# More units of a two-layer MLP computed with joined 512-column passes

## The chip, the cores and the metric

The kernel runs on 1 core of one Trainium2 chip. The metric is the device time of one execution in microseconds (us). Three executions of the kernel before took 1423.88, 1424.63 and 1425.09 us; the median is 1424.63 us.

The engines are called PE (TensorE: matrix products), PEld (its weight loads), DVE (VectorE), ACT (ScalarE), POOL (GpSimd) and SP (SyncE, which issues transfers).

## The reference

The program is a decoder trunk of two layers over 512 tokens of 1024 channels, all in float32. Each layer has a token mixer (a recurrence with pooling in the first, a Conformer convolution in the second), a cross-attention into 256 memory tokens, and a gated MLP. The change concerns the MLP:

```python
def conv_ffn(x, norm, w_up, dw_w, dw_b, w_down):
    h = rms_norm(x, norm) @ w_up                 # 1024 -> 2 * 3072
    g = causal_dwconv(h[..., :D_FF], dw_w, dw_b) # width 3, along the tokens
    u = h[..., D_FF:]
    return (jax.nn.gelu(g) * u) @ w_down         # 3072 -> 1024

for layer in range(DEPTH):                       # DEPTH = 2
    x = x + mixer(x); x = x + cross_attn(x, mem); x = x + conv_ffn(x)
return rms_norm(x, final_norm)
```

## The kernel before

**Split operands.** A float32 number is held as two parts, a rounded high part and the rest (low). A product of a weight block and an activation is three matmuls that add into one PSUM bank: high weight by high activation, high weight by low activation, low weight by high activation (`mm3`, L187 to L189).

**Units.** The up projection of the MLP makes 24 pairs of 128 channels, one gate row and one value row each; a pair is called a unit, c = 0 to 23. Units 0 and 1 are plain. Units 2 to 23 use a seven-product scheme (Strassen's, in Winograd's form): the 512 tokens are halved into two times 256, the 1024 input channels into two times 512, and seven products of a 128x512 weight block with a 512x256 activation block take the place of eight. The weight blocks are named a11, a12, a22, s1, s2, s3, s4 (the s are sums of blocks); the activation blocks are B11, B21, B22 and four combinations T1 to T4. The products add into three PSUM tiles: G takes a11 and a12; F takes a copy of a11's result (L992) and then s2, s3 and a22; H takes s1 and s4. Between two products ACT and DVE take the running value of F out of the bank.

On PE the order of a unit c is: s1, s2, a12, s3, then the down projection for units that were finished four to seven units ago (24 matmuls of 512 columns into tiles named `aux`, from unit 4 on), then a11 of the next unit (`ahead`), then s4 and a22. Units 2 and 3 have no down projection between s3 and a11.

**Narrow and joined products.** In a narrow unit each product is 12 matmuls of 256 columns: for each of four 128-channel chunks the three of `mm3`. In a joined unit (the code says wide, `WIDE` at L42) the products into F and G are made in `product` (L817) with 8 matmuls: for each chunk one of 512 columns, the high weights by the high and low activations side by side, and one of 256 columns, the low weights by the high activations. The two column halves of the bank are added afterwards (`gather`, L955 on ACT and L172 on DVE). H has 256 columns in both cases, and lies in the tile `stat` in joined units, in a tile `mm` in narrow ones.

**The re-laying copies.** A joined product needs the high and the low half of an activation block side by side. T1 to T4 are built so. B11, B21 and B22 are not; ACT re-lays them once a layer with copies of 128x256 (L217, four per block). `put_aside` first copies the high half of B22 to a spare place (4 copies), `put_beside(B21)` then writes the low half of B21 where B22's high half stood, `put_beside(B22)` puts B22 together, and `put_beside(B11)` does B11. From `put_aside` on, the product s4 reads B22's high half from the spare place. Where these calls stand is set by `WIDE[0]`, the first joined unit: aside and B11 two units ahead of it, B21 and B22 one unit ahead.

**Order.** Within the MLP the order of PE, ACT, DVE and POOL is the order of the code (`manual_schedule`). `finish`, which ends the second layer (down projection of the last four units in 384 columns, final norm), is ordered by the framework's scheduler up to its last part. The end of unit 23 is a chain on DVE and ACT: F and H times the norm (L963, L931 narrow; L961, L969 joined), convolution (L939, L942 twice), gelu (L944), product with the value row (L976), split (L979 high, L981 low). `finish` then multiplies the last result.

Of the kernel before, what the change touches and what calls it, by code (L numbers as in the profile page):

```python
# [24 lines left out]
CF = D_FF // P  # L25
# [13 lines left out]

KE = 2  # L40
PARKED = 4
WIDE = range(6, 22)  # L42
READY = 8
WINDOWS = (2, 4, 8, 16)

# [17 lines left out]
def trunk(ctx: ExitStack, tc: tile.TileContext, I: dict, out: list):  # L63
# [32 lines left out]
    def tmp_f(n=T):  # L96
        return tmp.tile([P, n], F32, tag="tmp", name=nm("tmp"))
# [73 lines left out]
    def add(out, a, b):  # L171
        V.tensor_tensor(out, a, b, op=ALU.add)  # L172
        return out
# [703 lines left out]
        return {c: Blocks(I["wpair"][layer * (CF - PLAIN) + c - PLAIN]) for c in range(PLAIN, CF)}  # L877

    def ffn(layer, norm, nxt, seven, pairs):
        ys = {}  # L880

        class Down:

# [11 lines left out]
            def bank(self, i, seeded):  # L895

                ps = aux_ps()
                if seeded:
                    A.activation(ps, X[2 * self.j + i], AF.Copy)
                return ps  # L900
# [16 lines left out]
        def high(c, name):  # L917
            if c in pairs and (c, name) not in done:
                pairs[c].high(name)

        def low(c, name):
            if c in pairs and (c, name) not in done:
                pairs[c].low(name)
                done.add((c, name))

        def both(c, name):
            high(c, name)
            low(c, name)

        def times_r(out, ps, at):  # L930
            V.tensor_tensor(out[:, at], ps, norm.r[:, at], op=ALU.mult)  # L931
# [13 lines left out]
            yield y  # L945

        def wide(c):
            return c in WIDE

        def bank(c):  # L950
            return main_ps() if wide(c) else main_ps()[:, :M]

        def gather(out, ps):

            A.activation(out, ps[:, M:], AF.Copy)  # L955
            add(out, ps[:, :M], out)
# [26 lines left out]
        def m(c, ps, block, j, first=True):  # L983
            seven.product(ps, pairs[c].w[block], j, first)

        def ahead(c):

            G, F = bank(c), bank(c)
            m(c, G, "a11", seven.B11)
            if c == WIDE[0] + 1:  # L990
                PE.matmul(F, pairs[c].w["a11"][0][:, :P], seven.both(seven.B11, 0), start=True, stop=True)
            A.activation(F, G, AF.Copy)  # L992
            return G, F

        def unit(c):

            nonlocal left, chains
            G, F = chains
            down, seeded = downs.get(c), c > GC
            H = (stat_ps if wide(c) else main_ps)()[:, :M]  # L1000
            m(c, H, "s1", seven.T1)
            if c <= second:
                high(c + 1, "s3")
            next(left, None)
            if c <= second:
                low(c + 1, "s3")

            m(c, F, "s2", seven.T2, False)
            u, f, g = tmp_f(), tmp_f(), tmp_f()
            if wide(c):  # L1010
                gather(u[:, :M], F)
            else:
                A.activation(u[:, :M], F, AF.Copy)
            if c == first:
                both(c + 2, "a11")
            if down:
                d = [down.bank(i, seeded) for i in range(2)]
            next(left, None)
            both(c + 1, "s3")
            next(left, None)  # L1020
            high(c + 1, "a22")

            m(c, G, "a12", seven.B21, False)
            next(left, None)
            next(left, None)
            high(c, "s4")
            if c == second:
                high(c + 2, "a11")
            low(c, "s4")
            if wide(c):  # L1030
                gather(g[:, left_half], G)
            elif c > second:
                times_r(g, G, left_half)

            m(c, F, "s3", seven.T3, False)
            if wide(c):
                gather(u[:, M:], F)
            else:
                A.activation(u[:, M:], F, AF.Copy)
            add(f[:, right_half], H, u[:, M:])  # L1040
            if c <= second:
                times_r(g, G, left_half)
            if c == second:
                low(c + 2, "a11")
            low(c + 1, "a22")
            if not wide(c):
                V.tensor_tensor(f[:, right_half], f[:, right_half], norm.r[:, right_half], op=ALU.mult)
            both(c + 2, "a11")
            high(c + 1, "a12")
            low(c + 1, "a12")  # L1050
            if c == WIDE[0] - 2:
                seven.put_aside()
            elif c == WIDE[0] - 1:
                seven.put_beside(seven.B21)
            if down:
                for ks in (range(GC - 1), (GC - 1,)):
                    for i in range(2):
                        down.products(i, d[i], seeded, ks)
            if c + 3 in pairs:
                pairs[c + 3].load()  # L1060
            if c + 2 in pairs and c > first:
                pairs[c + 2].load_second()
            if c > second and c + 1 in downs:
                downs[c + 1].w.high()
                downs[c + 1].w.low()
            if c + 2 in downs and first < c <= CF - 2:
                downs[c + 2].load()
            high(c + 1, "s1")
            low(c + 1, "s1")
            high(c + 1, "s2")  # L1070
            low(c + 1, "s2")
            if c == second:
                downs[c + 1].w.high()
                downs[c + 1].w.low()
            if down:
                down.home(0, d[0], seeded)

            if c + 1 in pairs:
                chains = ahead(c + 1)
            if down:  # L1080
                down.home(1, d[1], seeded)
            if c == WIDE[0] - 2:
                seven.put_beside(seven.B11)

            m(c, H, "s4", seven.B22, False)
            m(c, F, "a22", seven.T4, False)
            if c == WIDE[0] - 1:
                seven.put_beside(seven.B22)
            left = gating(c, g, f, u, F, H)
            next(left)  # L1090

        def opening():
# [67 lines left out]

            start(3)
            chains = ahead(first)

            def rest():
# [14 lines left out]
        with tc.manual_schedule(engines=ORDERED):  # L1179
            opening()  # L1180
            for c in range(PLAIN, CF):
                unit(c)
            for _ in left:
                pass
# [714 lines left out]
    six = mixer(n0, n1)  # L1899
    pairs = pairs_of(0)  # L1900
    mem, parked = ffn(0, n2, n3, attention(0, n1, mem, n2, six, pairs[PLAIN]), pairs)
    six = conformer(n3, n4, mem, parked)
    pairs = pairs_of(1)
    ffn(1, n5, None, attention(1, n4, mem, n5, six, pairs[PLAIN]), pairs)


# [76 lines left out]
```

## Time and profile before

| What | Value |
|---|---|
| median of three executions | 1424.63 us |
| the profiled execution, its own time | 1424.63 us |
| its span, first to last instruction | 1422.8 us |
| PE busy | 1411.7 us, 99% |
| ACT busy | 934.0 us, 66% |
| DVE busy | 1115.0 us, 78% |
| granted clock of PE, mean | 0.999 of full speed |

The span is 1.8 us shorter than the time. The busy time of PE counts matmuls from start to a modelled end, and they overlap in the pipeline, so 99% says that PE has few gaps and not that it could not issue faster. How closely matmuls follow each other is read from their start times. The MLP of the first layer lies between 340 and 620 us of the span, that of the second from 1040 us on.

### The profile page before, as it was taken

The numbers are of one execution on the slowest core, as the hardware profiler recorded it, in microseconds if no ns is written. First come the engines' busy times: TensorE is split into PE (matmuls) and PEld (weight loads), VectorE is DVE, ScalarE is ACT, GpSimd is POOL, SyncE is SP. The second block draws the span as 40 slices with busy tenths as digits, with TensorE's granted clock in tenths as the row PEclk, the third lists the DMA queues.
The fourth block names the chain that finished last, engine by engine and source line by source line (L and its number), as shares of the span: only waits on it lengthen the run. The fifth ranks groups of instructions, "written<-read, shape, count | busy, mean of one in ns | idle before, by whom it ended". The sixth has DMA issues, their size and how long they took to land.

```text
span 1422.8 us, 21779 instructions
## 1 busy us (share of the span) xinstructions
PE 1411.7 (99%) x8012; PEld 1228.3 (86%) x8012; DVE 1115.0 (78%) x1860; ACT 934.0 (66%) x1688; POOL 316.8 (22%) x333
## 2 busy tenths in 40 slices
PE   9999999999999999999999999999999999999998
PEld 7988888998898888888988777899889888888897
DVE  6987776778877777777798997968788777777775
ACT  7578744777576676666665547766756766666664
POOL 0011310110122222222008993011002222222211
PEclk9999999999999999999999999999999999999999
DMA  8623232544387777776442454345438777777741
GB/s 302 198 75 103 91 118 82 114 116 135 97 205 168 173 172 170 171 173 168 134 133 89 119 158 153 105 88 133 112 98 193 180 176 165 176 174 167 175 122 60
DMA packets 80027, 204.26 MB, mean 144 GB/s; under 512 B 9008, under 2 KB 9520, under 8 KB 79920
## 3 DMA queue, kind: packets, MB, share of 16 engines
q1 hardware_dynamic: 50832, 150.15, 32.5%
q0 software_dynamic: 28800, 52.44, 21.5%
q8 instruction: 63, 1.03, 0.3%
q14 instruction: 44, 0.36, 0.1%
q10 hardware_dynamic: 288, 0.27, 0.1%
HBM read 145.16 MB, written 2.10 MB: 103 GB/s over the span
## 4 chain that ended last, share of the span: by engine, by line
PE 92%; DVE 2%; POOL 2%; DMA 1%; issue 1%; ACT 1%; SPq 0%; POOLq 0%; DVEq 0%; ACTq 0%
PE mm L817 16%; PE mm L187 15%; PE mm L188 15%; PE mm L189 15%; PE aux L187 7%; PE aux L188 7%; PE aux L189 7%; PE stat L187 2%; PE stat L189 2%; PE stat L188 2%; PE mm L465 2%; DMA raw<-in_wv 1%; POOL actf L1583 1%; DVE wlo L168 1%; PE aux L539 0%
## 5 line engine op out<-in xcount | busy, mean ns | idle before, releaser
L188 PE MATMUL mm<-act,whi 128*128 128x512 f32 (+2 forms) x805 | 296.8, 369 | 0.3 <-DVE act L182 0.2
L187 PE MATMUL mm<-act,whi 128*128 128x512 f32 (+2 forms) x805 | 296.6, 370 | 0.6 <-ACT act L281 0.6
L189 PE MATMUL mm<-act,wlo 128*128 128x512 f32 (+2 forms) x805 | 296.6, 368 | 0.0
L187 PEld LDWEIGHTS mm<-act,whi 128*128 128x128 f32 x805 | 151.5, 188 | 26.8 <-ACT act L281 0.9
L188 PEld LDWEIGHTS mm<-act,whi 128*128 128x128 f32 x805 | 151.7, 188 | 26.0 <-DVE act L168 1.0
L189 PEld LDWEIGHTS mm<-act,wlo 128*128 128x128 f32 x805 | 151.6, 188 | 25.1 <-DVE wlo L168 0.6
L866 DVE TENSOR_TENSOR bigr<-raw,bigr 128x512 fp32r<-128x512 f32 x176 | 120.7, 687 | 61.0 <-ACT bigr L859 57.3
L187 PE MATMUL aux<-act,whi 128*128 128x512 f32 x399 | 155.6, 390 | 0.0
L188 PE MATMUL aux<-act,whi 128*128 128x512 f32 x399 | 155.5, 390 | 0.0
L189 PE MATMUL aux<-act,wlo 128*128 128x512 f32 x399 | 155.3, 389 | 0.0
L859 ACT ACTIVATE bigr<-raw 128x512 fp32r<-128x512 f32 x176 | 109.4, 623 | 68.7 <-DVE wlo L204 66.2
L872 POOL DMA_DIRECT2D raw<-wa x100 | 87.3, 893 | 299.7 <-DVE bigr L866 189.8
L167 ACT ACTIVATE whi<-raw 128x1024 fp32r<-128x1024 f32 (+1 forms) x95 | 96.5, 1020 | 85.8 <-PE mm L188 45.7
L817 PE MATMUL mm<-bigr,bigr 128*128 128x512 f32 (+1 forms) x768 | 150.6, 338 | 0.0
L817 PEld LDWEIGHTS mm<-bigr,bigr 128*128 128x128 f32 x768 | 118.3, 189 | 14.3
L869 POOL DMA_DIRECT2D raw<-raw x50 | 43.2, 864 | 371.6 <-DVE wlo L866 297.6
L172 DVE TENSOR_TENSOR tmp<-mm,tmp 128x256 f32<-128x256 f32 x194 | 77.8, 417 | 40.4 <-ACT tmp L955 37.9
L168 DVE TENSOR_TENSOR wlo<-raw,whi 128x1024 fp32r<-128x1024 f32 (+1 forms) x75 | 90.3, 1209 | 19.0 <-ACT whi L167 18.3
L817 PE MATMUL mm<-act,whi 128*128 128x512 f32 x256 | 95.5, 396 | 0.0
L189 PEld LDWEIGHTS aux<-act,wlo 128*128 128x128 f32 x399 | 74.9, 188 | 15.9
L188 PEld LDWEIGHTS aux<-act,whi 128*128 128x128 f32 x399 | 74.9, 188 | 15.5
L187 PEld LDWEIGHTS aux<-act,whi 128*128 128x128 f32 x399 | 75.0, 188 | 14.2
(378 smaller groups left out, 3505.5 us busy)
## 6 DMA issues: line engine op xcount, KB each, us to landing
raw<-wa POOLq DMA_DIRECT2D x150, 256.0 KB, 3.4
wa<-in_wpair SPq DMA_DIRECT2D x88, 256.0 KB, 3.8
raw<-in_wpair SPq DMA_DIRECT2D x44, 512.0 KB, 3.8
big<-in_wdown SPq DMA_DIRECT2D x42, 512.0 KB, 4.6
raw<-raw POOLq DMA_DIRECT2D x50, 256.0 KB, 4.1
raw<-in_pw SPq DMA_DIRECT2D x24, 512.0 KB, 3.4
raw<-in_win SPq DMA_DIRECT2D x20, 512.0 KB, 3.3
raw<-in_wk SPq DMA_DIRECT2D x16, 512.0 KB, 3.3
```

The costliest lines, as they stand in the source:

```text
L167: A.activation(hi, src, AF.Copy)
L168: fetched[1] = (eng or V).tensor_tensor(lo, src, hi.bitcast(F32), op=ALU.subtract)
L172: V.tensor_tensor(out, a, b, op=ALU.add)
L187: PE.matmul(ps, wh, xh, start=first, stop=False, skip_group_check=onto)
L188: PE.matmul(ps, wh, xl, start=False, stop=False, skip_group_check=onto)
L189: return PE.matmul(ps, wl, xh, start=False, stop=last, skip_group_check=onto)
L465: PE.matmul(p, m[j], x, start=k == 0 and j == 0 and x is hi, stop=k == C - 1 and x is lo)
L817: PE.matmul(to, part, by, start=first and c == 0 and i == 0, stop=c == 3 and i == 1, skip_group_check=True)
L859: A.activation(self.w[name][0], self.block(name), AF.Copy)
L866: V.tensor_tensor(lo, self.block(name), hi.bitcast(F32), op=ALU.subtract)
L869: G.dma_start(self.r, self.z, accum_op=ALU.add)
L872: G.dma_start(block, self.a22, accum_op=ALU.add)
```

## The change

`WIDE` becomes one range per layer. Unit 5 becomes a joined one in both layers, and units 22 and 23 also in the second layer. So four units change from narrow to joined, and the re-laying copies, whose place follows `WIDE[0]`, move from units 4 and 5 to units 3 and 4. One matmul that opens a bank moves from unit 7's a11 to unit 6's.

```diff
-WIDE = range(6, 22)
+WIDE = range(5, 22), range(5, CF)
...
-        ys = {}
+        ys, wides = {}, WIDE[layer]
...
         def wide(c):
-            return c in WIDE
+            return c in wides
...
-            if c == WIDE[0] + 1:
+            if c == wides[0] + 1:
                 PE.matmul(F, pairs[c].w["a11"][0][:, :P], seven.both(seven.B11, 0), start=True, stop=True)
...
-            if c == WIDE[0] - 2:
+            if c == wides[0] - 2:
                 seven.put_aside()
-            elif c == WIDE[0] - 1:
+            elif c == wides[0] - 1:
                 seven.put_beside(seven.B21)
...
-            if c == WIDE[0] - 2:
+            if c == wides[0] - 2:
                 seven.put_beside(seven.B11)
...
-            if c == WIDE[0] - 1:
+            if c == wides[0] - 1:
                 seven.put_beside(seven.B22)
```

The first place where the order changes is ACT in unit 3 of the first layer. The names: `whi_3801` is unit 4's a12, `bigr_3984` and `bigr_3987` (in the changed kernel `bigr_3990`, `bigr_3993`) are unit 4's s1 and s2, `mm_3996` is F of unit 4. Before:

```order
L1039 ACTIVATE tmp_3925<-mm_3850 128x256
L859 ACTIVATE whi_3801<-wa_3651 128x512
L859 ACTIVATE bigr_3984<-raw_3647 128x512
L859 ACTIVATE bigr_3987<-raw_3647 128x512
L201 ACTIVATE whi_3991<-big_3653 128x1024
L992 ACTIVATE mm_3996<-mm_3995 128x256
L939 ACTIVATE tmp_4036<-tmp_3927,par 128x512
```

The same place in the changed kernel:

```order
L1039 ACTIVATE tmp_3925<-mm_3850 128x256
L859 ACTIVATE whi_3801<-wa_3651 128x512
L217 ACTIVATE act_3976<-act_3264 128x256
L217 ACTIVATE act_3976<-act_3337 128x256
L217 ACTIVATE act_3977<-act_3438 128x256
L217 ACTIVATE act_3977<-act_3540 128x256
L859 ACTIVATE bigr_3990<-raw_3647 128x512
L859 ACTIVATE bigr_3993<-raw_3647 128x512
L201 ACTIVATE whi_3997<-big_3653 128x1024
L992 ACTIVATE mm_4002<-mm_4001 128x256
L217 ACTIVATE act_3251<-act_3252 128x256
L217 ACTIVATE act_3297<-act_3298 128x256
```

The four copies of `put_aside` stand behind a12's split, and those of B11 behind the copy of a11's result.

PE in the same unit: the product s4 of unit 3 (`mm_3892` is H, `bigr_3949` the weight block), with the semaphores that an instruction waits for. Before:

```order
L189 MATMUL mm_3995<-act_3500,wlo_3802 128x256
L187 MATMUL mm_3892<-act_3264,bigr_3949 128x256 [waits DVE_49]
L188 MATMUL mm_3892<-act_3265,bigr_3949 128x256
L189 MATMUL mm_3892<-act_3264,bigr_3949 128x256
L187 MATMUL mm_3892<-act_3337,bigr_3949 128x256
L188 MATMUL mm_3892<-act_3338,bigr_3949 128x256
```

In the changed kernel:

```order
L189 MATMUL mm_4001<-act_3500,wlo_3802 128x256
L187 MATMUL mm_3892<-act_3976,bigr_3949 128x256 [waits DVE_49,Activation_49]
L188 MATMUL mm_3892<-act_3265,bigr_3949 128x256
L189 MATMUL mm_3892<-act_3976,bigr_3949 128x256
L187 MATMUL mm_3892<-act_3976,bigr_3949 128x256 [waits Activation_49]
L188 MATMUL mm_3892<-act_3338,bigr_3949 128x256
L189 MATMUL mm_3892<-act_3976,bigr_3949 128x256
L187 MATMUL mm_3892<-act_3977,bigr_3949 128x256 [waits Activation_49]
```

It now reads the copies, and each chunk has a wait for ACT of its own.

The third place is the end of the second layer on ACT (`tmp_14417`, in the changed kernel `tmp_14351`, is unit 23's gate row; L1222 takes transposed channels of x out of PSUM for `finish`). Before:

```order
L904 ACTIVATE x<-aux_14322 128x512
L939 ACTIVATE tmp_14417<-tmp_14318,par 128x512
L944 ACTIVATE tmp_14417<-tmp_14417 128x512
L1222 ACTIVATE big_14450<-aux_14480 128x512
L979 ACTIVATE act_14424<-tmp_14417 128x512
```

In the changed kernel:

```order
L904 ACTIVATE x<-aux_14267 128x512
L939 ACTIVATE tmp_14351<-tmp_14262,par 128x512
L955 ACTIVATE tmp_14261<-mm_14199 128x256
L1222 ACTIVATE big_14386<-aux_14416 128x512
L944 ACTIVATE tmp_14351<-tmp_14351 128x512
L979 ACTIVATE act_14360<-tmp_14351 128x512
```

A gather has come in, and L1222 has moved ahead of the gelu.

On PE, at the same end, `finish` reads the last result (`act_14424`, in the changed kernel `act_14360`) for the first time after the four transposes of L1221. Before, seven matmuls stand between:

```order
L1221 MATMUL aux_14480<-ident,x 128x128 x4
L187 MATMUL mm_14492<-act_14011,whi_14431 128x384
L188 MATMUL mm_14492<-act_14012,whi_14431 128x384
L189 MATMUL mm_14492<-act_14011,wlo_14432 128x384
L187 MATMUL mm_14492<-act_14180,whi_14431 128x384
L188 MATMUL mm_14492<-act_14181,whi_14431 128x384
L189 MATMUL mm_14492<-act_14180,wlo_14432 128x384
L187 MATMUL mm_14492<-act_14338,whi_14431 128x384
L187 MATMUL mm_14451<-act_14424,whi_14385 128x384
L187 MATMUL mm_14467<-act_14424,whi_14385 128x384
L188 MATMUL mm_14492<-act_14339,whi_14431 128x384
```

In the changed kernel eighteen stand there, nine into `mm_14428` and nine into `mm_14445`; these are the last of them and what follows:

```order
L187 MATMUL mm_14445<-act_14137,whi_14367 128x384
L188 MATMUL mm_14445<-act_14138,whi_14367 128x384
L189 MATMUL mm_14445<-act_14137,wlo_14368 128x384
L187 MATMUL mm_14387<-act_14360,whi_14323 128x384
L187 MATMUL mm_14403<-act_14360,whi_14323 128x384
L187 MATMUL mm_14428<-act_14360,whi_14367 128x384
L187 MATMUL mm_14445<-act_14279,whi_14367 128x384
L188 MATMUL mm_14387<-act_14361,whi_14323 128x384
```

The first matmul with the last result stands eleven matmuls later than before.

## Rows read from the trace of the kernel before

**Rows 1.** The page: busy time by engine, and the chain's shares by engine.
```profile
PE 1411.7 (99%) x8012; PEld 1228.3 (86%) x8012; DVE 1115.0 (78%) x1860; ACT 934.0 (66%) x1688; POOL 316.8 (22%) x333
...
PE 92%; DVE 2%; POOL 2%; DMA 1%; issue 1%; ACT 1%; SPq 0%; POOLq 0%; DVEq 0%; ACTq 0%
```

**Rows 2.** Stretches: length, busy time (instructions) per engine, granted clock, DMA share, GB/s.
```profile
404.92:420.46 15.54, 15.54 (x110) 14.58 (x109) 11.80 (x21) 11.80 (x26) 3.44 (x4) 1.00 0.84 189
451.43:466.77 15.34, 15.34 (x89) 13.50 (x88) 11.80 (x21) 10.40 (x21) 3.44 (x4) 1.00 0.66 162
1365.95:1381.49 15.54, 15.54 (x111) 14.58 (x109) 10.41 (x18) 8.38 (x16) 1.72 (x2) 1.00 0.40 102
```

**Rows 3.** Timeline of PE, units 4 and 5: start, duration (us), instruction.
```profile
410.39 0.28 PE L187 MATMUL mm<-act,whi 128*128 128x256 f32 x1
...
420.46 0.40 PE L187 MATMUL aux<-act,whi 128*128 128x512 f32 x1
```

**Rows 4.** Timeline of ACT, unit 3 of the first layer.
```profile
395.56 0.62 ACT L859 ACTIVATE whi<-wa 128x512 fp32r<-128x512 f32 x1
396.09 0.62 ACT L859 ACTIVATE bigr<-raw 128x512 fp32r<-128x512 f32 x1
397.92 0.63 ACT L859 ACTIVATE bigr<-raw 128x512 fp32r<-128x512 f32 x1 [1.22 <-PE mm L189]
...
399.41 0.37 ACT L992 ACTIVATE mm<-mm 128x256 f32<-128x256 f32 x1
401.75 0.81 ACT L939 ACTIVATE tmp<-tmp,par 128x512 f32<-128x512 f32 x1 [1.98 <-DVE tmp L963]
```

**Rows 5.** Timeline of ACT, unit 4: copies and what follows them.
```profile
409.11 1.33 ACT L217 ACTIVATE act<-act 128x256 fp32r<-128x256 f32 x4
410.34 1.05 ACT L201 ACTIVATE whi<-big 128x1024 fp32r<-128x1024 f32 x1
```

**Rows 6.** Groups of DVE by line and form: count, busy us, mean ns, idle before.
```profile
L961 DVE TENSOR_TENSOR tmp<-tmp,r 128x512 f32<-128x512 f32 x32 | 22.1, 692 | 1.1
...
L963 DVE TENSOR_TENSOR tmp<-tmp,r 128x256 f32<-128x256 f32 x12 | 5.1, 424 | 0.4
```

**Rows 7.** Timeline of all engines where s4 of unit 3 begins, first layer.
```profile
395.70 0.42 DVE L172 TENSOR_TENSOR tmp<-mm,tmp 128x256 f32<-128x256 f32 x1
...
396.18 0.19 PEld L187 LDWEIGHTS mm<-act,bigr 128*128 128x128 f32 x1
396.18 0.39 PE L187 MATMUL mm<-act,bigr 128*128 128x256 f32 x1
```

**Rows 8.** The same place in the second layer.
```profile
1080.36 0.19 PEld L187 LDWEIGHTS mm<-act,bigr 128*128 128x128 f32 x1
```

**Rows 9.** Timeline of PE in `finish`.
```profile
1394.44 0.94 PE L187 MATMUL mm<-act,whi 128*128 128x384 f32 x3
1395.22 0.33 PE L188 MATMUL mm<-act,whi 128*128 128x384 f32 x1
1395.39 0.33 PE L189 MATMUL mm<-act,wlo 128*128 128x384 f32 x1
```

**Rows 10.** Timelines of ACT and DVE at the end of unit 23, second layer.
```profile
1390.17 0.81 ACT L939 ACTIVATE tmp<-tmp,par 128x512 f32<-128x512 f32 x1 [1.60 <-DVE tmp L963]
1394.08 0.62 ACT L979 ACTIVATE act<-tmp 128x512 fp32r<-128x512 f32 x1
...
1391.02 1.54 DVE L942 SCALAR_TENSOR_TENSOR tmp<-tmp,par,tmp 128x511 f32<-128x511 f32 x2 [0.55 <-ACT tmp L939]
```

**Rows 11.** Timelines of DVE, ACT and PE in joined unit 20, second layer.
```profile
1347.01 1.53 DVE L942 SCALAR_TENSOR_TENSOR tmp<-tmp,par,tmp 128x511 f32<-128x511 f32 x2
1348.45 0.42 DVE L172 TENSOR_TENSOR tmp<-mm,tmp 128x256 f32<-128x256 f32 x1
...
1344.83 0.82 ACT L939 ACTIVATE tmp<-tmp,par 128x512 f32<-128x512 f32 x1 [0.33 <-DVE tmp L961]
...
1349.06 0.74 PE L817 MATMUL mm<-bigr,bigr 128*128 128x512 f32 x3
```

## The prediction

> **What bounds the kernel now.** I read the page first. PE is busy 1411.7 us of 1422.8, and the chain that ended last runs for 92% through PE [rows 1]. So the question is how fast PE issues, and which waits open a gap on it. Next I read the stretches that hold one unit each, from the first matmul of one unit's down projection to the first of the next [rows 2]. In all of them PE is busy the whole time at a granted clock of 1.00, that is 2.4 GHz, while ACT is busy 8.38 to 11.80 us and DVE 10.41 to 11.80 us of some 15.4. ACT and DVE have slack on average, PE has none: a unit lasts as long as PE takes to issue its matmuls. A narrow unit takes 15.54 us in either layer, a joined one 15.34. The timeline gives the same at finer grain: 84 matmuls of 256 columns start between 410.39 and 420.46 [rows 3], one every 0.120 us. Last I looked for the places where the changed order lets PE wait: s4 of unit 3, and the first use of the last result in `finish`.
>
> **Part 1: four units become joined.** Each loses 20 matmuls (five products of 12 become five of 8); the columns streamed stay 3072 a product. The load counts of the stretches, 109 against 88, show these 20 and one instruction of the stretch's edge [rows 2]. The worth is 15.54 - 15.34 = 0.20 us a unit; unit 5 twice and units 22 and 23 once make 4 x 0.20 = 0.80 us. It cannot be much more, as the columns remain. The added work is three gathers (ACT and DVE) and wider multiplications by the norm. It costs nothing inside units 5 and 22, because joined units with the same additions already run with PE busy throughout. If that cover were gone it would show as rival 3.
>
> Here a rule speaks against the change. The rows give 0.20 us for 20 matmuls, or 10 ns for one left out. The Trainium skill (TensorE: Matmul & The Clock Gate, "Wait — 56ns, not 53.3ns?") says that a warm matmul takes its columns at 2.4 GHz and about 2.5 ns more. By that rule 20 matmuls fewer would be worth 0.05 us a unit, 0.2 us in all, an estimate from that page; the trace does not agree with it for these loads and shapes, as 0.120 us for 256 columns leaves 13 ns above 107. The sum goes by the rows; the rule is rival 4.
>
> **Part 2: the copies one unit sooner.** In units 4 and 5 they had time: a down projection stands between s3 and s4 there. In unit 3 none does, and s4 now reads what `put_aside` writes. On ACT the copies stand behind a12's split (395.56, 0.62 us); the instruction after it started at 396.09 [rows 4], so the first copy starts there. Four copies take 1.33 us and the next instruction starts 1.23 us after the first [rows 5]: one starts every 0.31 us, and the first lasts 1.33 - 3 x 0.31 = 0.41 us. So it ends at 396.50.
>
> PE loads s4's first weights at 396.18 before the change [rows 7]. This was itself the end of a wait: the DVE instruction that reads H (395.70, 0.42 us) ended at 396.12, and the load followed 0.06 us later. With the same 0.06 us the load comes at 396.56, which is 0.38 us later. The next chunk follows 3 x 0.12 = 0.36 us behind, its copy only 0.31 us, so each later chunk finds its copy ready: I take one wait of 0.38 us. The second layer has the same pattern (load at 1080.36) [rows 8]. Together +0.76 us. Bounds: nothing, if ACT runs somewhat ahead of PE there; and 1.3 us a layer, if PE waits for the fourth copy. I take 0.38 because the changed order gives each chunk its own wait.
>
> What the copies push: the split of s1 (396.09) moves 1.23 us back, but ACT sat idle for 1.22 us after it, so the split of s2 at 397.92 stays [rows 4]. s1's block is read only after s4 and a22, 24 matmuls or 2.9 us after s4's start. The four copies of B11 fit into ACT's idle 1.98 us before L939 [rows 4]. Behind PE's new wait queue all later matmuls, a loss that nothing gives back, since PE has no slack. SP and POOL keep their order; no transfer is added. Unit 4 keeps eight copies, now B21's and B22's, in the places of those it had; unit 5 loses its eight.
>
> **Part 3: the end.** Before, `finish` waits for the last result: three matmuls of 384 columns take 1395.22 - 1394.44 = 0.78 us where the pitch is 0.17 [rows 9], a loss of 0.26 us. L979 made that operand by 1394.70 [rows 10]. The joined end is a longer chain. L961 takes 0.69 us against 0.42 for L963 [rows 6]: +0.27. From L939 to L942 it takes 1347.01 - 1344.83 = 2.18 us in a joined unit [rows 11] against 1391.02 - 1390.17 = 0.85 us at the narrow end [rows 10], for the gather waits behind L939 on ACT: +1.33. So the operand comes 1.60 us later, near 1396.3. But its first use stands eleven matmuls later in the changed order, 11 x 0.17 = 1.9 us. The wait should shrink from 0.26 us to little; I take -0.20. Bounds: -0.26, and +0.30 if the chain grows by 0.56 us more than I think (L1222, now ahead of the gelu, could do that, though the transposes that it waits for come well before the gelu's input).
>
> **Sum.** -0.80 + 0.76 - 0.20 = -0.24 us on the profiled execution, whose own time of 1424.63 us is the median of the three. That gives 1424.4 us, with 1424.0 to 1424.9 as this case's own range.
>
> **Rivals.**
>
> 1. The copies are hidden, ACT being early enough, so that s4 doesn't wait longer. Then -0.80 - 0.20 = -1.0: 1423.6 us. For it: the wait is 0.38 us only, little against the spread of an instruction's start. Against: both layers show the same pattern with PE and ACT level to a tenth of a us [rows 4, 7, 8].
> 2. The other side: s4 of unit 3 waits for the last copy and not the first. The copies end at 396.09 + 1.33 = 397.42, the load comes at 397.48, 1.3 us late, in two layers 2.6 us: -0.80 + 2.6 - 0.20 = +1.6, or 1426.2 us. It decides from 0.5 us a layer on, where the wait eats the 1.0 us of gains. For it: ACT might start the copies late if a12's split is late. Against: the waits stand chunk by chunk.
> 3. The chains of joined units collide. In unit 20 DVE ends the gather of F at 1348.45 + 0.42 = 1348.87, and s3, which writes that bank again, starts at 1349.06 [rows 11]: some 0.1 us to spare. Units 6, 22 and 23 now run behind a joined unit, four places over both layers. If each waits 0.25 us, the sum is -0.24 + 1.0: 1425.4 us. Against: units 8 to 21 run so already without a gap.
> 4. The joined passes are worth less than the stretches say, because most of the 0.20 us between them comes from something else, such as fewer copies and splits on the memories beside PE. If a quarter is left, -0.2 + 0.76 - 0.20 = +0.36, or 1425.0 us. Against: the narrow stretch of unit 22's end has ACT and DVE far less busy (8.38 and 10.41 us) than that of unit 4's (11.80 both), and both take 15.54 us [rows 2]. The rule of the Trainium skill in Part 1 (TensorE: Matmul & The Clock Gate) would leave about that quarter.
>
> **How the numbers follow.** Chances: forecast 0.56, rival 1 0.12, rival 2 0.15, rival 3 0.10, rival 4 0.07. The three executions of before spread from 1423.88 to 1425.09, so a median can move by some 0.4 us by itself. The range is 1423.1 to 1426.2 us: it takes in rivals 1, 3 and 4 with that spread, and reaches rival 2. About what a measurement of this kernel can tell from no change is 0.2%, 2.8 us. No case reaches it; only several errors of one sign would. Faster 0.03, within 0.94, slower 0.03.
>
> **What would show it.** In the changed profile: 80 matmuls fewer; stretches of units 5 (both layers), 22 and 23 (second layer) of 15.34 instead of 15.54 us; in unit 3 of each layer the first weight load of s4 about 0.06 us behind the end of the first L217 and some 0.4 us later than its place in the stream of matmuls; no other new gap on PE in the two MLPs; and in `finish` hardly a gap where the last result is first used. I am wrong if s4 of unit 3 waits over 0.5 us or not at all, if PE gaps appear before s3 of units 6, 22 or 23, or if the end of `finish` is late by more than 0.3 us.

## The result, and the profile after

The changed kernel takes 1429.42 us, the median of 7 runs (1426.64 to 1430.19), against 1424.45 us of the kernel before, run beside it (7 runs, 1423.05 to 1425.09). The ratio is 1.0034, with an interval of 1.0025 to 1.0043: 5 us slower, where 0.2 us faster was forecast. The profiled execution took 1426.64 us, the fastest of the seven, 2.0 us more than the one of before. So 3 of the 5 us are not in this profile.

The page of the changed kernel, busy times and the chain's shares [rows 1]:

```profile
PE 1410.6 (99%) x7932; PEld 1223.7 (86%) x7932; DVE 1120.2 (79%) x1868; ACT 937.0 (66%) x1696; POOL 316.8 (22%) x333
...
PE 85%; DVE 4%; issue 3%; DMA 3%; ACT 2%; POOL 2%; SPq 0%; POOLq 0%; ACTq 0%; DVEq 0%
```

80 matmuls went and PE is busy 1.1 us less, but the span grew: PE idles 3.2 us more. The chain leaves PE oftener (85% against 92%), and DMA and "issue" grow in it. The stretches [rows 2] from the down projection of unit 4 to that of unit 5 in the first layer, and from that of unit 22 to that of unit 23 in the second (both took 15.54 us before):

```profile
404.41:419.80 15.39, 15.39 (x94) 13.72 (x93) 12.06 (x22) 11.77 (x26) 3.44 (x4) 1.00 0.84 191
...
1366.53:1381.87 15.34, 15.34 (x89) 13.55 (x88) 11.80 (x20) 9.20 (x18) 1.72 (x2) 1.00 0.42 105
```

So the joined units run nearly as forecast: 15.34 to 15.39 us at a full clock. Where s4 of unit 3 begins, first PE, then ACT [rows 4, 7]:

```profile
395.19 0.28 PE L189 MATMUL mm<-act,wlo 128*128 128x256 f32 x1
395.67 0.39 PE L187 MATMUL mm<-act,bigr 128*128 128x256 f32 x1 [0.20 <-ACT act L217]
395.89 0.28 PE L188 MATMUL mm<-act,bigr 128*128 128x256 f32 x1
```
```profile
394.69 0.62 ACT L859 ACTIVATE whi<-wa 128x512 fp32r<-128x512 f32 x1
395.21 1.33 ACT L217 ACTIVATE act<-act 128x256 fp32r<-128x256 f32 x4
396.43 0.63 ACT L859 ACTIVATE bigr<-raw 128x512 fp32r<-128x512 f32 x1
```

The next matmul starts 0.48 us after the one ahead instead of 0.12: 0.36 us, once a layer, for the first copy alone. The first use of the last result in `finish` [rows 9, 10], PE and then ACT:

```profile
1396.18 0.34 PE L189 MATMUL mm<-act,wlo 128*128 128x384 f32 x1
1397.10 0.62 PE L187 MATMUL mm<-act,whi 128*128 128x384 f32 x2 [0.58 <-ACT act L979]
```
```profile
1387.81 1.06 ACT L167 ACTIVATE whi<-raw 128x1024 fp32r<-128x1024 f32 x1 [0.32 <-DMA raw<-in_wdown]
...
1396.42 0.63 ACT L979 ACTIVATE act<-tmp 128x512 fp32r<-128x512 f32 x1 [0.76 <-DVE tmp L976]
```

The wait did not shrink; it grew from 0.26 to 0.85 us, and ahead of it ACT waits for a load of down weights. Transfers are late elsewhere too. The issues by group (count, KB each, median us from issue to landing), before and after:

```profile
raw<-in_win SPq DMA_DIRECT2D x20, 512.0 KB, 3.3
raw<-in_wk SPq DMA_DIRECT2D x16, 512.0 KB, 3.3
...
last<-big SPq DMA_DIRECT2D x1, 256.0 KB, 2.3
last<-big ACTq DMA_DIRECT2D x1, 256.0 KB, 2.6
```
```profile
raw<-in_win SPq DMA_DIRECT2D x20, 512.0 KB, 3.7
raw<-in_wk SPq DMA_DIRECT2D x16, 512.0 KB, 3.7
...
last<-big SPq DMA_DIRECT2D x1, 256.0 KB, 3.5
last<-big ACTq DMA_DIRECT2D x1, 256.0 KB, 3.7
```

Loads that the change does not touch take 0.4 us longer, and the two last stores some 1.1 us longer. By the start of the same PE instruction in both traces, the profiled difference of +2.0 us is made up so:

| stretch | us |
|---|---|
| start, first attention (waits for first loads, -1.0 to +1.2 among the profiles without idle matmuls at the start) | -0.87 |
| first MLP (one wait of 0.36 us; joined unit -0.17) | +0.24 |
| last down weights of the first MLP, matmul at 712 us | +0.59 |
| conformer, second attention | +0.21 |
| second MLP (waits of 0.36 and 0.39 us; joined units) | +0.21 |
| end of `finish`: the last result | +0.63 |
| from there to the end: the last stores | +1.00 |

The ACT row behind the third line, after the change; before, the idle time ahead was 1.41 us:

```profile
708.45 1.06 ACT L167 ACTIVATE whi<-raw 128x1024 fp32r<-128x1024 f32 x1 [2.00 <-DMA raw<-in_wdown]
```

### The profile page after: what moved, and what is told of

Read it like the earlier page. It is cut to its first block, busy times and chain, and to the rows that moved or that the text cites. A ratio compares the mean times of both kernels' runs of the same rounds, so it can differ in the third digit from the quotient of the medians.

```text
span 1424.9 us, 21640 instructions
## 1 busy us (share of the span) xinstructions
PE 1410.6 (99%) x7932; PEld 1223.7 (86%) x7932; DVE 1120.2 (79%) x1868; ACT 937.0 (66%) x1696; POOL 316.8 (22%) x333
## 4 chain that ended last, share of the span: by engine, by line
PE 85%; DVE 4%; issue 3%; DMA 3%; ACT 2%; POOL 2%; SPq 0%; POOLq 0%; ACTq 0%; DVEq 0%
PE mm L817 17%; PE mm L187 12%; PE mm L188 12%; PE mm L189 12%; PE aux L187 7%; PE aux L188 7%; PE aux L189 7%; PE stat L187 2%; PE stat L189 2%; PE stat L188 2%; PE mm L465 2%; DMA raw<-in_wv 1%; DVE wlo L168 1%; DMA raw<-wa 1%; ACT whi L167 1%
## 5 line engine op out<-in xcount | busy, mean ns | idle before, releaser
L187 PE MATMUL mm<-act,whi 128*128 128x512 f32 (+2 forms) x773 | 287.2, 373 | 1.7 <-ACT act L979 1.1
L188 PE MATMUL mm<-act,whi 128*128 128x512 f32 (+2 forms) x773 | 287.8, 372 | 0.3 <-DVE act L182 0.2
L189 PE MATMUL mm<-act,wlo 128*128 128x512 f32 (+2 forms) x773 | 287.5, 372 | 0.0
L817 PE MATMUL mm<-bigr,bigr 128*128 128x512 f32 (+1 forms) x864 | 169.5, 339 | 0.1
L187 PEld LDWEIGHTS mm<-act,whi 128*128 128x128 f32 x773 | 145.4, 188 | 27.9 <-ACT act L979 1.9
L188 PEld LDWEIGHTS mm<-act,whi 128*128 128x128 f32 x773 | 145.6, 188 | 25.9 <-DVE act L168 1.0
L189 PEld LDWEIGHTS mm<-act,wlo 128*128 128x128 f32 x773 | 145.5, 188 | 25.0 <-DVE wlo L168 0.6
L817 PEld LDWEIGHTS mm<-bigr,bigr 128*128 128x128 f32 x864 | 133.0, 189 | 16.5 <-DVE tmp L172 0.4
L172 DVE TENSOR_TENSOR tmp<-mm,tmp 128x256 f32<-128x256 f32 x202 | 80.9, 417 | 43.2 <-ACT tmp L955 41.4
L817 PE MATMUL mm<-act,whi 128*128 128x512 f32 x288 | 107.4, 396 | 0.0
L955 ACT ACTIVATE tmp<-mm 128x256 f32<-128x256 f32 x144 | 49.8, 371 | 67.5 <-PE mm L817 67.5
L188 PEld LDWEIGHTS aux<-act,whi 128*128 128x128 f32 x399 | 74.9, 188 | 15.7
```

The lines of the kernel that those rows point to most:

```text
L187: PE.matmul(ps, wh, xh, start=first, stop=False, skip_group_check=onto)
L188: PE.matmul(ps, wh, xl, start=False, stop=False, skip_group_check=onto)
L189: return PE.matmul(ps, wl, xh, start=False, stop=last, skip_group_check=onto)
L817: PE.matmul(to, part, by, start=first and c == 0 and i == 0, stop=c == 3 and i == 1, skip_group_check=True)
```

## The experiments

Each changes one or two places of the changed kernel or of the kernel before. "From 30 us on" below means the span's difference to the profile of before, less the difference that was there at 30 us; it is +3.0 us for the changed kernel's profile.

**e1 to e4: the parts.** Unchanged again; the sixth units alone; the last two alone; unit 22 alone.

```diff
-WIDE = range(5, 22), range(5, CF)
+WIDE = range(5, 22), range(5, 22)     # e2
+WIDE = range(6, 22), range(6, CF)     # e3
+WIDE = range(6, 22), range(6, 23)     # e4
```

> The changed kernel once more, unchanged, for a second profile beside its times. Theory A (the end of the second layer: the joined last unit makes a longer chain, and the last transfer of the down weights and the last gather stand in it): the profile shows a PE gap of 1 us or more before the first use of the last result in finish, and the time is 1427 to 1430 us. Theory B (unit 5: joined behind an unseeded unit 4, s3 waits for the gather on DVE, and the copies wait at s4 of unit 3): gaps of 0.3 to 1.5 us at s4 of unit 3 and s3 of unit 5 in both layers, which vary from run to run, and the end as in the first profile.

> Only unit 5 joined in both layers (and the copies one unit sooner); units 22 and 23 of the second layer stay narrow. Theory A: the loss is in the end, so this one takes 1424.5 to 1425.2 us (two waits of 0.4 us, one of 0.4 us at s3 of unit 5, less 0.4 us of gain). Theory B: it takes most of the loss, 1427 to 1429 us.

> Only units 22 and 23 of the second layer joined; unit 5 narrow and the copies where they were. Theory A: 1427 to 1429.5 us, with the PE gap in finish. Theory B: 1424.0 to 1425.0 us (0.4 us of gain, 0.6 us of wait at the end).

> Only unit 22 of the second layer joined, unit 23 narrow, unit 5 narrow. Theory A (it is the chain of the last unit that costs): as before or 0.2 us faster, 1424.2 to 1424.6 us, and the end of the trace as before. If joined unit 22 itself costs (its gathers stand in unit 23, where the weights for finish are split): 1425.5 us or more.

Against 1424.33 of before: e1 1428.91 (ratio 1.002 to 1.0045), e2 1425.56 (0.9997 to 1.0014), e3 1423.82 (0.9987 to 1.0005), e4 1424.14 (0.999 to 1.0008). Neither part carries the excess: +1.2 and -0.5 alone (neither clear of the scatter), +4.6 together. Both theories fell. In e2 and e3 the loads of in_wk take 3.4 and 3.3 us and the last store 2.3 and 2.8; the 2.8 us of e3 stay open, as no instruction fetch falls into that store.

**e5, e6: the sixth unit of one layer, with the last two.** `range(5, 22), range(6, CF)` and `range(6, 22), range(5, CF)`.

> The sixth unit joined in the first layer alone, the last two of the second layer as in the changed kernel. Alone, the two sixth units cost +1.2 us (1425.56 against 1424.33) and the last two gave -0.5 (1423.82), together +4.5. Theory E (place of an instruction fetch: in the changed kernel the 8 KB fetch of queue 14 that starts 1421.71 shares a DMA engine with the packets of the last store, which end 1422.67; ACT and DVE have 8 and 9 instructions more, so it falls earlier than in the kernels that add 4): with 6 and 7 more it falls between, about 1 us behind the last store; the store is not delayed and the time is 1424 to 1425 us. Theory F (the second layer's sixth unit and the last two hinder each other): no such pair here, 1424 to 1424.6 us. Theory G (either layer's sixth unit does it): half of the excess, 1426 to 1427 us.

> The second layer alone changed: sixth unit and last two joined, the first layer as before. Theory E (place of an instruction fetch): the same 6 and 7 instructions more as with the first layer's sixth unit, so the same time as that kernel within 0.5 us, 1424 to 1425 us, and the last store not delayed. Theory F (the second layer's sixth unit and the last two hinder each other): the whole excess is here, 1428 to 1429.5 us. Theory G: half of the excess, 1426 to 1427 us.

1427.07 (1.001 to 1.0027) and 1426.11 (1.0005 to 1.0023). The last store is in time (2.4 us in both), as theory E said, but both are 1 to 2 us slower than it allows, whichever layer: the loads are long (3.8 and 3.7 us) in both.

**e7, e8: moving the last fetch.** In the changed kernel an instruction fetch of 8 KB starts at 1421.71, and the last store's packets that should end near 1421.9 end at 1422.67. The transfers between 1421.3 and 1423 us by queue (packets, MB, share of 16 DMA engines):

```profile
q10 hardware_dynamic: 98, 0.17, 28.0%
q1 hardware_dynamic: 24, 0.02, 3.0%
q14 instruction: 1, 0.01, 1.1%
```

```diff
             left = gating(c, g, f, u, F, H)
             next(left)
+            if layer == 0 and 10 <= c < 18:
+                A.activation(pad, eps, AF.Copy)     # e7; e8: V.tensor_copy(pad, eps)
```

Here and below `pad` stands for a spare tile of one column.

> The changed kernel with 8 more instructions on ACT, copies of one column into a spare tile, one in each of units 10 to 17 of the first layer, where ACT is busy 12 of 15 us. They compute nothing that is used. Theory E, if the late fetch is ACT's: it comes about 8 ACT instructions (some 5 us) earlier and misses the last store; the two last stores land 2.3 and 2.7 us behind their issue as before the change, not 3.5 and 3.7, and the time falls by 1.0 us or more, to 1428 or less against 1429. If the fetch is DVE's, nothing changes: 1429 us. Theory H (the excess is a wait in the order of the work): 1429 us, up to 0.3 more.

> The changed kernel with 8 more instructions on DVE, copies of one column into a spare tile, one in each of units 10 to 17 of the first layer. They compute nothing that is used. Theory E, if the late fetch is DVE's: it comes some 5 us earlier, misses the last store, and the time falls by 1.0 us or more, to 1428 or less; of this kernel and the one with ACT's 8 exactly one moves the fetch. If it is ACT's: 1429 us. Theory H (the excess is a wait in the order of the work): 1429 us, up to 0.3 more, in both.

e7 1428.71 (1.002 to 1.004), its last stores 3.3 and 3.6 us; e8 1427.25 (1.0011 to 1.0028), 2.4 and 2.7 us, its fetch at 1413.44. So the fetch is DVE's: the nine DVE instructions that the change adds bring it onto the last store. That is 1.0 us in the traces, 1.5 us between the medians of e7 and e8, whose intervals overlap. The other 3 us stayed.

**e9 to e12: is it the length of DVE's or ACT's program?** Idle copies in the kernel before, instructions left out of the changed kernel.

```diff
+                for _ in range(2): V.tensor_copy(pad, eps)                   # e9, on the kernel before
+                A.activation(pad, eps, AF.Copy)                              # e10, on the kernel before
-            for s in (1, 2):
+            for s in (1,) if layer == 0 and 10 <= c < 18 else (1, 2):        # e11
-            A.activation(y, y, AF.Gelu_apprx_tanh)
+            if not (layer == 0 and 10 <= c < 18): A.activation(y, y, ...)    # e12
```

> The kernel before with 16 more DVE instructions, copies of one column into a spare tile that nothing reads, two in each of units 10 to 17 of the first layer; 2379 DVE instructions instead of 2363, no unit joined. In the profiles so far the loads of in_wk take 3.25 to 3.37 us (median of 16) in the kernels of up to 2368 DVE and 1910 ACT instructions (before, sixth units, last two, unit 22), and 3.68 to 3.83 us in those with 2370 or more and 1912 or more, whatever the order of the work. Theory I (the length of DVE's program decides it): loads of in_wk near 3.75 us, the wait for the last down weights of the first layer (matmul at 712 us) 0.6 us or more, time 1425.5 to 1427 us. Theory J (ACT's length decides): loads near 3.3 us, 1424.4 us. Theory H (the order of the joined units is all of it): 1424.4 us and loads as before.

> The kernel before with 8 more ACT instructions of the same idle kind, one in each of units 10 to 17 of the first layer: 1914 ACT instructions as the changed kernel has, DVE's 2363 as before. Theory J (ACT's length decides how long loads take): loads of in_wk near 3.75 us, 1425.5 to 1427 us. Theory I (DVE's length) and theory H (the order): loads near 3.3 us, 1424.4 us.

> The changed kernel without the second tap of the gate's convolution in units 10 to 17 of the first layer: 8 DVE instructions fewer, 2364, where DVE has slack. It leaves out that part of the computation. Theory I with the end's fetch: loads of in_wk near 3.3 us; the last fetch falls behind the last store, which lands 2.3 us after its issue; time 1424.4 to 1425.5 us, 4 us below the changed kernel. Theory J: the fetch alone goes, 1427.5 to 1428 us, loads near 3.75 us. Theory H: 1429 us, as the joined units are all there.

> The changed kernel without the gelu in units 10 to 17 of the first layer: ACT has 1898 instructions instead of 1914, DVE its 2372. It leaves out that part of the computation. Theory J (ACT's length): loads of in_wk near 3.3 us, the last store still late by 1.0 us, time 1426.5 to 1427.5 us. Theory I (DVE's length) and theory H: loads near 3.75 us, 1428.5 to 1429.5 us.

1424.6 (0.999 to 1.0008), 1425.28 (0.9994 to 1.0011), 1427.52 (1.0011 to 1.0028), 1428.02 (1.0015 to 1.0035). Loads of in_wk: 3.34, 3.36, 3.85, 3.79 us. Theories I and J both fell: the loads stay with the kernel. e11 again frees the last store (2.4 us). Over all runs of the five kernels with 7932 matmuls whose last stores are held up (after, e1, e7, e12, e16) the median is 1428.59 us, over those of the two where they are not (e8, e11) 1427.49: 1.1 us, as in the traces.

**e13 to e16: PE's number of instructions.** What all kernels with long loads share is few matmuls. e13 and e14 give them back as idle ones at the start, e15 takes matmuls from the kernel before, e16 lengthens the program on POOL.

```diff
-    for _ in range(10):
-        PE.matmul(idle[:, :P], onesf, onesf, start=True, stop=True)
+    for _ in range(35):                                                      # e13, e14 (with e8's copies)
+        PE.matmul(idle[:, :32], onesf, onesf[:, :32], start=True, stop=True)
-            m(c, H, "s4", seven.B22, False)
+            if not (layer == 0 and 10 <= c < 16): m(c, H, "s4", ...)         # e15, on the kernel before
+                for _ in range(10): nc.gpsimd.memset(pad, 0.0)               # e16
```

> The changed kernel with 35 idle matmuls of 32 columns at the start instead of 10 of 128, while PE waits for its first weights: 50 more matmuls in the trace, 7982 instead of 7932. Theory K (the number of PE's instructions decides how long loads of in_wk and in_wdown take): loads of in_wk near 3.3 us (median of 16), the wait at the first layer's last down weights back to some 0.15 us, the last store still late; time 1426.5 to 1427.5 us, 2 us below the changed kernel; up to 0.5 us of it may be lost at the start. Theory L (the length of the whole program decides): the program is longer by 100 instructions, so the same. Theory H (the order of the joined units, or chance): loads near 3.75 us, 1429 us.

> As the kernel with the idle matmuls, and 8 idle DVE copies besides, one in each of units 10 to 17 of the first layer, which moved the last instruction fetch off the last store before. Theory K: loads of in_wk near 3.3 us and the last store 2.3 us after its issue: 1425 to 1426 us, so that the waits of the joined units (0.8) and the start (0.5) are all that is left above the kernel before. Theory H: 1427.3 us, as with the DVE copies alone.

> The kernel before without the fourth product (s4, 12 matmuls of 256 columns) in units 10 to 15 of the first layer: 7940 matmuls in the trace instead of 8012. It leaves out that part of the computation; 72 x 0.120 = 8.6 us of PE's work go. Theory K (PE's number) and theory L (the whole program's length): loads of in_wk near 3.75 us, and the time falls by only 6.5 to 7.5 us, to 1417 to 1418 us. Theory H: loads near 3.3 us, 1415.8 us.

> The changed kernel with 80 idle memsets of one column on POOL, 10 in each of units 10 to 17 of the first layer; PE as in the changed kernel, 7932 matmuls, the whole program 80 instructions longer than the changed kernel's and at about the length of the sixth-units kernel, which has the short loads. Theory L (whole length): loads of in_wk near 3.3 us, 1427 us. Theory K (PE's number): loads near 3.75 us, 1429 us. POOL is busy for a fifth of the time, but its DMAs may come up to 0.3 us later.

The groups of in_wk in e13, e15 and e16:

```profile
raw<-in_wk SPq DMA_DIRECT2D x16, 512.0 KB, 3.3
```
```profile
raw<-in_wk SPq DMA_DIRECT2D x16, 512.0 KB, 3.7
```
```profile
raw<-in_wk SPq DMA_DIRECT2D x16, 512.0 KB, 3.8
```

For the length of the loads theory K held in both directions, and L and H fell. In all 20 profiles:

| matmuls in the trace | kernels | loads of in_wk, median us | fetches on queue 8 |
|---|---|---|---|
| 8012 | before, e9, e10 | 3.30 to 3.36 | 63 |
| 7972 to 7992 | e2, e3, e4, e13, e14, e17, e18 | 3.25 to 3.37 | 63 |
| 7932 to 7952 | after, e1, e5 to e8, e11, e12, e15, e16 | 3.68 to 3.85 | 62 |

The last column counts instruction fetches of 16 KB, which follow PE's program: the idle matmuls of e17 below add one. The split falls exactly where there is one fetch less (in e2 the 63rd starts after the span's end). The pages of before and after:

```profile
q8 instruction: 63, 1.03, 0.3%
```
```profile
q8 instruction: 62, 1.02, 0.3%
```

The times were missed, first by a side effect. e13 took 1435.64 us and e14 1434.9 (1.007 to 1.0098 and 1.0064 to 1.0091), because each idle matmul took 0.213 us at the start, where the clock is at its lower level (until 19.7 us in e13, 4.5 in the changed kernel), and the work began 11.2 us later than in the changed kernel's profile. From 30 us on e13 is at +0.6 us and e14 at -1.1, against +3.0 of the changed kernel: 2.4 us less, and 1.7 more in e14, of which the freed last store is 1.0 (0.7 between the two medians).

Not all of the 2.4 us is the length of the loads. 0.5 us lie at the load of 708.45 and 0.4 in `finish`; 1.4 lie between 716 and 1040 us, 1.2 of them in one wait of PE for DVE at 862 us. Here it is in before, after and e13:

```profile
PE stat L305 <- DVE actf L1598: 1.5, 1, 1.5
```
```profile
PE stat L305 <- DVE actf L1598: 1.8, 1, 1.8
```
```profile
PE stat L305 <- DVE actf L1598: 0.6, 1, 0.6
```

It is 0.5 to 0.9 us in the seven kernels of the table's second row and 1.4 to 2.3 us in all others, also in the three with 8012 matmuls, whose loads are short. So the length of the loads does not decide it alone, and what does stays open. Here is the ACT row of e14 that answers to the one at 708.45:

```profile
719.03 1.06 ACT L167 ACTIVATE whi<-raw 128x1024 fp32r<-128x1024 f32 x1 [1.43 <-DMA raw<-in_wdown]
```

e15 took 1423.79 us (0.9995, 0.9987 to 1.0004), not 1417: its first MLP is 3.6 us shorter, not 8.6, as PE then waits for DVE; behind it 2.1 us are lost again, 0.6 of them at the load of the last down weights and most of the rest in waits before unit 4 of the second MLP. Its waits of PE:

```profile
PE stat L305 <- DVE actf L1599: 2.3, 1, 2.3
PE mm L817 <- DVE tmp L172: 1.4, 6, 0.2
```

The second row is rival 3's place, six waits in six units: with s4 gone these units take 14.65 us, set by DVE, so in a joined unit of 15.34 us DVE's chain has only some 0.7 us to spare. e16 took 1428.49 (1.0019 to 1.0042).

**e17, e18: the idle matmuls at the end.**

```diff
             fifth = last(3)
+            idle = stat_ps()
+            for _ in range(56):
+                PE.matmul(idle[:, :32], ones, ones[:, :32], start=True, stop=True)   # e18 with e8's copies
```

> The changed kernel with 56 idle matmuls of 32 columns behind PE's last matmul (which ends 1416.9 of 1424.9), 7988 in all. Nothing that is used waits for them. Theory K (PE's number of instructions sets the length of the loads of in_wk and in_wdown): loads of in_wk near 3.3 us; from 30 us on the kernel with the matmuls at the start was 2.6 us less late than at 30 us, so the time is 2 to 4 us below the changed kernel: 1425 to 1427 us, the last store perhaps still late. Rival (it was the longer start, which moved everything, and not the number): loads near 3.75 us, 1429 us.

> The same with the 8 idle DVE copies in units 10 to 17 of the first layer, which move the last DVE fetch off the last store. Theory K with the fetch: 1424 to 1426 us, 0.5 to 1 us below the kernel with the idle matmuls alone, and within 1 us of the kernel before (1424.4); what is left is the waits of the joined units against their gain. Rival: 1427.3 us, as with the DVE copies alone.

The loads are short (3.31 and 3.29 us), the times only 1428.22 (1.0014 to 1.0032) and 1427.26 (1.0011 to 1.0029) against 1424.93. The expectation held for the loads and failed for the time. Measured against the changed kernel's trace, they win 1.0 and 1.2 us between 30 and 1013 us and 0.4 us more at the end. But a 16 KB fetch for the idle matmuls starts at 1422.05 and 1421.31 while the last stores are under way, and they take 3.5 and 3.7 us in both, also in e18, where DVE's fetch is gone from there. The load of the last down weights ahead of 712 us takes 4.4 and 4.5 us, though the others are short, and PE waits 1.1 us at 712 us. The profile of e17 has the waits of the next paragraph, 2.5 us; in that of e18 the span ends 3.2 us after the last landing, not 1.6. Why the load and e18's end are late is not shown.

**What differs from profile to profile.** In the second MLP, PE's waits in units 3 to 5 together (time between starts beyond the usual pitch) are 0.1 to 0.44 us in the seven profiles with a narrow sixth unit there. In the 13 with a joined one they are 0.46 to 0.84 us in seven, 1.36 in e18, and 2.2 to 2.5 us in e2, e8, e11, e16 and e17; the mean is 1.3. ACT in unit 3 of the second layer, e16 and then e6:

```profile
1084.59 0.63 ACT L859 ACTIVATE bigr<-raw 128x512 fp32r<-128x512 f32 x1 [1.96 <-DMA raw<-wa]
...
1086.07 0.37 ACT L992 ACTIVATE mm<-mm 128x256 f32<-128x256 f32 x1
```
```profile
1083.74 0.63 ACT L859 ACTIVATE bigr<-raw 128x512 fp32r<-128x512 f32 x1 [0.34 <-PE mm L189]
```

In e16 the split of s2 waits for an adding transfer of POOL (a DMA that adds one weight block to another), and the copy L992 that PE waits for stands behind it. Three transfers issued within 1.5 us, in e16 and in e6:

```profile
big<-in_wdown SPq DMA_DIRECT2D x1, 512.0 KB, 7.1
raw<-wa POOLq DMA_DIRECT2D x1, 256.0 KB, 7.4
wa<-in_wpair SPq DMA_DIRECT2D x1, 256.0 KB, 4.6
```
```profile
big<-in_wdown SPq DMA_DIRECT2D x1, 512.0 KB, 5.2
raw<-wa POOLq DMA_DIRECT2D x1, 256.0 KB, 3.8
wa<-in_wpair SPq DMA_DIRECT2D x1, 256.0 KB, 4.0
```

SP issues its two loads when an earlier adding transfer lands. Where that is over 1.0 us after POOL's issue (e6, e13, e14), POOL's transfer takes 3.7 to 3.8 us; 0.5 to 0.8 us after (before, e3, e4, e15) 4.2 to 5.3; within 0.45 us 5.4 to 7.6 us. The Trainium skill (DMA: Bandwidth & Descriptors, "Issuing engines are not separate DMA queues") says that transfers of all issuing engines run on the same 16 DMA engines and interleave. The traces agree: the transfer takes twice as long when the others start with it (7.4 us in e16, 3.8 in e6).

## Why the prediction was wrong, step by step

**What bounds the kernel: right, and too narrow.** PE's issue sets the length of the units. But the waits in which PE stands elsewhere, at loads, and the landing of the last stores were taken as fixed, since "SP and POOL keep their order; no transfer is added". That is the step that failed first: the sum has no term for transfers, and the traces show +1.0 us at the last stores, +0.6 us at 712 us and 0.4 us of the +0.63 in `finish`. The second is Part 3, whose sign was wrong.

**Part 1, right.** Forecast -0.80. From the first to the last stretch around unit 5 the profiled gain is 46.51 - 46.34 = 0.17 us in the first layer, and units 22 and 23 give (15.49 + 15.54) - (15.38 + 15.34) = 0.31 us: with unit 5 twice, some -0.65. The sum's 0.20 us a unit was somewhat large. The rule that would have left a quarter (rival 4; the Trainium skill, TensorE: Matmul & The Clock Gate, "Wait — 56ns, not 53.3ns?") would give 0.05 us a unit, an estimate from that page; the trace gives about 0.16.

**Part 2, right for the copies.** s4 of unit 3 waits 0.36 us longer in every profile that joins unit 5, in either layer; 0.38 was forecast. Rivals 1 and 2 fall. What the step left out is behind them: the gather of unit 5 comes late on DVE, rival 3's mechanism but in unit 5, where none of its four places was: 0.35 to 0.39 us in the first layer in three of the 13 profiles that join unit 5 there, up to 0.81 us in the second. And with the transfer above late, in five profiles, s2 of unit 4 waits 0.9 to 1.2 us in the second layer.

**Part 3, wrong: -0.20 forecast, +0.63 measured.** Two numbers failed. The operand came 1.96 us later, not 1.60 (L979 starts 14.55 us after the last down projection begins, before 12.59): the chain's own part is right, 1.53 us in e3, where no load is waited for; 0.4 us is the long load of the third down weights. And the first use moved 1.36 us (1396.36 - 1381.87 against 1394.62 - 1381.49), not 1.9: eight matmuls, not eleven, as the trace has fifteen and not eighteen between the transposes and the first use. 1.96 - 1.36 = 0.60 us. The prediction had named an end late by more than 0.3 us as a sign of being wrong.

**What no step had.** "No transfer is added" was true and said nothing of instruction fetches. DVE's last one moved onto the last store: +1.0 us in the traces (e8 and e11 take it away, e7 does not). PE's smaller number of instructions goes with loads that are 0.4 us longer: 0.6 us at 712 us and 0.4 in `finish`, against the kernel before. In the conformer the changed kernel is only 0.2 us later than before; that e13 is 1.4 us earlier there than the changed kernel is not explained by the loads' length.

**Together.** Joined units -0.65; waits in units 3 to 5 +0.45 and +1.2 (first and second layer, the mean over the 13 profiles each that join unit 5; the changed kernel's own two are lower, 0.36 and 0.5 to 0.75); loads at 712 and the conformer +0.9; end +0.63; last store +1.0: +3.5 of the 4.6 to 5.0 us. So 1 us or more stays open: no profile fell on a run near 1430 us, and the start scatters by as much. The range, 1423.1 to 1426.2, was built on the MLPs and `finish` alone.

**What stays open.** Why loads are longer below 7972 matmuls was not found. The split in the table is complete and goes with one 16 KB fetch of PE's program, but how a shorter program could lengthen a load is not shown: between 7952 and 7972 nothing was run, and the trace does not show where programs and tensors lie in memory. What the longer loads cost is read from the traces and not shown by a median: e13 and e14 carry the offset of their start, and e17 and e18, with short loads, are not clearly faster than the changed kernel. e3 and e4, the fastest kernels here that leave nothing out, have that short wait at 862 us, and so gain 0.6 and 0.8 us in the conformer, where nothing of theirs differs from before: their -0.5 and -0.2 us are no proof for the joined units at the end. No version beat the kernel before by more than its uncertainty.

## What to carry to other kernels

When an expected gain is a few tenths of a microsecond in a kernel whose busiest engine hardly waits, list the places where engines wait for transfers and the last store, also far from the change: a changed number of instructions moves the fetches and can cost more than the edit gains (here 1.0 us at the last store against 0.65). Test that with idle instructions on one engine at a time, placed where the engine has slack, before explaining the time by the order of the work. And take several profiles: a race between two issues of transfers showed in five of thirteen.

## What the runs showed of the hardware that was not expected

- One 8 KB instruction fetch, begun while a store of 256 KB was under way, went with a landing after 3.5 us, against 2.4 us in e8, whose fetch falls elsewhere.
- A load of in_wk that runs alone (128 packets of 4 KB) takes 3.3 or 3.7 us by the program. Its slowest packet takes 0.5 to 0.7 us (medians by kernel) in those with short loads and 0.8 to 1.3 us in those with long ones.
- In e9's profile (1429.89 us; its median is 1424.6) PE stood for 1.5 us at 731.4, and the granted clock then fell to its lower level, 1.2 GHz, from 733.4 to 740.2 us; matmuls of 256 columns started every 0.213 instead of 0.120 us, and 4.3 us were lost in all, 1.3 of them in the longer wait itself. Before the fall and in the fall (length, busy PE, PEld, DVE, ACT, POOL, clock, DMA share, GB/s):

```profile
729.00:733.00 4.00, 2.46 (x22) 2.26 (x20) 2.08 (x4) 3.00 (x4) 0.00 (x0) 1.00 0.40 149
733.00:741.00 8.00, 8.00 (x40) 7.86 (x41) 3.60 (x9) 1.93 (x5) 0.00 (x0) 0.57 0.42 131
```
